# Token-major query/key products in a two-layer hybrid trunk, with the output sums queued behind the low parts

## The chip, the core and the metric

The kernel runs on one core of a Trainium2 chip. A core has a matrix engine (TensorE, PE in the profile, with its weight loads shown apart as PEld), a vector engine (VectorE, DVE), an activation engine (ScalarE, ACT), a general engine (GpSimd, POOL) and a sequencer that here only issues DMAs (SyncE, SP). Each engine takes its instructions in the order of its own queue and waits on semaphores for the others. The metric is the device time of one execution in microseconds; lower is better.

## What is computed

Two layers are applied to x, 512 tokens by 2048 features. Each layer normalises, projects with one wide matrix, runs two groups of heads on the parts of the projection, gates them, maps them back with an output matrix, normalises again and adds to the residual:

```python
h = rmsnorm(x, g_pre)
z = h @ w_in
gq, gk, gv, gg, ga, aq, ak, av, ag = split_columns(z)
log_a = jax.nn.log_sigmoid((ga @ w_alpha + b_alpha)) / GLA_TAU
o_gla = rmsnorm(gla_chunk_causal(gq, gk, gv, log_a)) * jax.nn.silu(gg)
o_att = rmsnorm(chunk_band_attention(aq, ak, av, rel_bias)) * jax.nn.silu(ag)
y = jnp.concatenate([o_gla, o_att], axis=-1) @ w_out
return x + rmsnorm(y, g_post)
```

The attention group has 8 heads of 128 features; a query sees its own 64-token chunk and the eight before it, so with 512 tokens all earlier chunks. The gated linear attention group has 4 heads with 128 key and 256 value features.

## The kernel before

**Operands in two parts.** A float32 operand is split into a rounded high part and the remainder, its low part: ScalarE copies it to the rounded type and VectorE subtracts (`split`). A product is the sum of three matmuls: high by high, high by low, low by high.

**Seven products instead of eight.** The weights come in blocks of 512 columns. A pair of blocks times the tokens is a two by two block product, and `fast_gemm` computes it with seven half-size products named P1 to P7, each over four chunks of 256 rows. The order of the 28 (product, chunk) steps is written out by hand (`PROD`, for the output `PROD_OUT` and `PROD_END`). The operands on the token side are sums of quarters: S1 (for P5), S2 (P6), S3 (P7) and S4 (P3). The operands on the weight side are formed on the way: for P5, P6 and P7 (and P4 of the output) `Job.high` adds or subtracts two weight quarters on VectorE (lines 185 and 187). Then ScalarE makes the high part `wh` (line 191) and VectorE the low part `wl` (line 199). `ahead` loads and prepares three to five steps in advance; `wh` has four buffers, `wl` three and `raw`, into which the weights land, four.

**Products of a layer, in order.** Two gate blocks with a plain product (AG); then by `fast_gemm` AV (values), two query/key pairs (the heads 0 to 3 and 4 to 7), KQ (the linear group's keys and queries), GV, GG, and the output blocks W01 and W23. In layer 0 W23 is a plain product. For a query/key pair (`feature_major=True`) the weights are the stationary operand and 256 tokens the moving one, so the result lies with features on partitions, as the scores want it; for the others 128 tokens are stationary and 512 weight columns moving.

**What fills the gaps.** While products are emitted, a `Pace` steps through a list of generators, `tasks`, at a written rate per step: attention (`attend`), the linear group, transposes of operands, `output_sums`. `until` steps them without a product between when a condition has to hold. A scheduler then sets the order on each engine from a timeline of its own, with the program's order as priority. `tc.issue_after(i)` gives it one more rule: what the block emits on the engine of `i` is queued after `i`, without a semaphore.

**At a query/key product's end** `qk_consume` forms the four results (`combine`, line 338, VectorE, for three; the fourth is read from PSUM as it is) and splits them; both heads of a pair are then handed to `attend`.

**The output product W01.** Its token-side sums are made by `output_sums`: S1 and S2 while GG and the first steps of W01 run, S4 after P5 and P6 have used their first chunks, S3 after their later ones (lines 1136 and 1153 with the splits at lines 105 and 106). `project` (lines 1280 and 1281) takes a finished result's squares on ScalarE and multiplies it by the gain on VectorE.

**The end.** In the last layer the residual of tokens 0 to 255, and of the first half of tile 2 (tokens 256 to 383), is added by a DMA: ScalarE scales the row (line 1305), GpSimd issues an accumulating DMA that adds `x_mid` to it (line 1306), and SyncE stores it (line 1307). The rest is updated by one VectorE instruction with the tokens held in SBUF (line 1311) and stored from SyncE and ScalarE in turn (line 1313).

Of the kernel before, what the change touches and what calls it, by code (L numbers as in the profile page):

```python
# [10 lines left out]
AF = mybir.ActivationFunctionType  # L11
# [22 lines left out]
def hybrid_trunk(  # L34
# [100 lines left out]
    last_cast = [None]  # L135

    class Job:
# [58 lines left out]
        def low(self):  # L196
            self.wl = rtile("wl", dtype=F32R, bufs=3)
            for z in self.parts():
                nc.vector.tensor_tensor(  # L199
                    out=self.wl[:, z, :], in0=self.src[:, z, :], in1=self.wh[:, z, :].bitcast(F32), op=ALU.subtract  # L200
                )
# [114 lines left out]
    def fast_gemm(l, pair, consume, rate=0.0, skip=0, feature_major=False, after=None, end=False, lag=0, ops=A):  # L316
# [38 lines left out]
        def matmuls(job, k, c, ts):  # L355
# [7 lines left out]
            for kk in range(2):  # L363
                if feature_major:
                    for ft in range(4):
                        f = slice(ft * P, (ft + 1) * P)
                        tok = slice(kk * 256, (kk + 1) * 256)
                        dst = out_ps[ft // 2][:, (ft % 2) * 256 : (ft % 2 + 1) * 256]
                        terms = ((job.wh, 0), (job.wh, 1), (job.wl, 0))
                        for m, (lhs, part) in enumerate(terms):  # L370
                            nc.tensor.matmul(  # L371
                                dst, lhs[:, kk, f], a[:, part, tok],
                                start=(fresh and kk == 0 and m == 0 and ft % 2 == 0),
                                stop=(c == 3 and kk == 1 and m == 2), skip_group_check=True,
                            )
                else:
                    for t in ts:
                        tok = slice(kk * 256 + t * P, kk * 256 + (t + 1) * P)
                        terms = ((0, job.wh), (0, job.wl), (1, job.wh))
                        for m, (part, rhs) in enumerate(terms):  # L380
                            nc.tensor.matmul(  # L381
                                out_ps[t], a[:, part, tok], rhs[:, kk, :],
                                start=(fresh and kk == 0 and m == 0),
                                stop=(c == 3 and kk == 1 and m == 2), skip_group_check=True,
                            )
# [302 lines left out]
    def layer(l):  # L688
# [274 lines left out]
        def qk_consume(p):  # L963
            sets = {}

            def f(j, h, b, src, comb):
# [454 lines left out]
```

## Time and profile before

| | us |
|---|---|
| median of three runs | 1648.65 (1648.48 to 1649.47) |
| profiled execution | 1642.34 |
| its span | 1640.5 |
| TensorE busy | 1617.2 |
| VectorE busy | 1253.5 |
| ScalarE busy | 909.7 |
| GpSimd busy | 134.2 |

The span runs from the first to the last instruction of the profiled execution; 1.84 us lie around it. The profiled execution is 6.31 us shorter than the median of the runs. In the trace the stages of a layer stand one after another on TensorE, so that a stretch of time belongs to one product; matmul instructions overlap, and the distance from one start to the next, not the length of one, is what a matmul costs.

### The profile page before, as it was taken

To read this page: it belongs to the slowest core of one execution; us is meant where nothing else is said; L and a number is where in the kernel's file an instruction comes from. 1 tells how busy PE (TensorE), PEld (TensorE's weight loads), DVE (VectorE), ACT (ScalarE), POOL (GpSimd) and SP (SyncE) were. 2 spreads that over 40 slices of the span, in tenths; PEclk is the share of its full clock that TensorE was granted. 3 is DMA by queue.
4 is the path that set the end of the run, shared out by engine and by line. 5 is a ranking of instruction groups with operands and counts; after the bars stand their busy time and mean duration, and the time that the engine had idled before them with its cause. 6 is when DMAs were issued, how large, how long until landed. Compare 5 with 4: busy or idle time off the path is not lost.

```text
span 1640.5 us, 24563 instructions
## 1 busy us (share of the span) xinstructions
PE 1617.2 (99%) x8986; PEld 1383.7 (84%) x8986; DVE 1253.5 (76%) x1635; ACT 909.7 (55%) x1498; POOL 134.2 (8%) x196
## 2 busy tenths in 40 slices
PE   9999999999999999999999999999999999999996
PEld 7888999998888778788888889999988877787885
DVE  5977677687787869985786576776777878699876
ACT  7554445566555456654784444455665545476554
POOL 0120000110100110000132000000000001101002
PEclk9999999999999999999999999999999999999998
DMA  9898685885859667486789486858758596786968
GB/s 345 270 357 293 221 302 199 266 298 173 307 192 339 225 220 267 145 296 214 240 282 394 172 311 218 298 189 273 269 183 291 184 327 235 241 282 246 345 224 269
DMA packets 130760, 426.70 MB, mean 260 GB/s; under 512 B 14084, under 2 KB 26756, under 8 KB 130640
## 3 DMA queue, kind: packets, MB, share of 16 engines
q1 hardware_dynamic: 113760, 366.09, 64.9%
q0 software_dynamic: 16304, 57.96, 9.7%
q8 instruction: 71, 1.16, 0.3%
q10 hardware_dynamic: 576, 1.08, 0.2%
q14 instruction: 49, 0.40, 0.1%
HBM read 371.84 MB, written 53.23 MB: 259 GB/s over the span
## 4 chain that ended last, share of the span: by engine, by line
PE 94%; DMA 2%; DVE 2%; issue 1%; ACT 0%; SPq 0%; DVEq 0%; POOL 0%; ACTq 0%
PE mm L381 47%; PE mm L371 19%; PE mm L302 16%; PE ax L891 2%; PE ax L381 2%; DMA raw<-in_w_dram 1%; PE ax L1072 1%; PE ax L874 1%; PE ax L711 1%; PE ax L1044 1%; DVE wl L199 1%; PE ax L855 1%; PE ax L854 1%; PE ax L853 1%; PE ax L1164 0%
## 5 line engine op out<-in xcount | busy, mean ns | idle before, releaser
L381 PE MATMUL mm<-wh,sa 128*128 128x512 f32 x1472 | 479.2, 396 | 1.2 <-ACT wh L191 1.0
L191 ACT CAST wh<-raw 128x1024 fp32r<-128x1024 f32 (+1 forms) x253 | 265.1, 1052 | 242.6 <-PE mm L381 65.2
L199 DVE TENSOR_TENSOR wl<-raw,wh 128x1024 fp32r<-128x1024 f32 (+1 forms) x253 | 306.5, 1216 | 92.7 <-PE mm L381 38.3
L191 ACT CAST wh<-H 128x1024 fp32r<-128x1024 f32 x240 | 251.4, 1050 | 214.8 <-PE mm L381 90.2
L199 DVE TENSOR_TENSOR wl<-H,wh 128x1024 fp32r<-128x1024 f32 x240 | 292.5, 1221 | 88.1 <-PE mm L381 35.8
L381 PEld LDWEIGHTS mm<-wh,sa 128*128 128x128 f32 x1472 | 277.5, 189 | 68.9 <-issue 7.9
L381 PE MATMUL mm<-wl,sa 128*128 128x512 f32 x736 | 289.6, 394 | 4.7 <-DVE wl L199 4.7
L371 PE MATMUL mm<-sa,wh 128*128 128x256 f32 x1280 | 236.7, 285 | 0.0
L381 PE MATMUL mm<-wh,a 128*128 128x512 f32 x608 | 200.5, 394 | 0.0
L371 PEld LDWEIGHTS mm<-sa,wh 128*128 128x128 f32 x1280 | 199.7, 191 | 0.1
L371 PE MATMUL mm<-sa,wl 128*128 128x256 f32 x640 | 181.2, 283 | 0.0
L381 PEld LDWEIGHTS mm<-wl,sa 128*128 128x128 f32 x736 | 139.1, 189 | 33.7 <-DVE wl L199 6.7
L185 DVE TENSOR_TENSOR H<-H,raw 128x1024 f32<-128x1024 f32 x132 | 160.2, 1219 | 8.1 <-DMA raw<-in_w_dram 7.0
L381 PEld LDWEIGHTS mm<-wh,a 128*128 128x128 f32 x608 | 113.2, 188 | 23.3
L187 DVE TENSOR_TENSOR raw<-H,raw 128x1024 f32<-128x1024 f32 x60 | 73.5, 1224 | 68.8 <-DMA raw<-in_w_dram 68.7
L371 PEld LDWEIGHTS mm<-sa,wl 128*128 128x128 f32 x640 | 122.5, 191 | 0.2
L421 POOL TENSOR_TENSOR sm<-sm,mhalf 128x2 f32<-128x2 f32 (+2 forms) x42 | 57.1, 1360 | 791.8 <-DVE sm L901 453.3
L381 PE MATMUL mm<-wl,a 128*128 128x512 f32 x304 | 119.8, 394 | 0.0
L371 PE MATMUL mm<-a,wh 128*128 128x256 f32 x512 | 95.2, 285 | 0.0
L302 PE MATMUL mm<-wh,a 128*128 128x512 f32 x288 | 91.7, 390 | 0.0
L381 PE MATMUL mm<-wh,g 128*128 128x512 f32 x288 | 90.8, 389 | 0.0
L333 ACT COPY ev<-mm 128x512 f32<-128x512 f32 x96 | 56.0, 583 | 56.3 <-PE mm L381 39.5
(237 smaller groups left out, 2428.5 us busy)
## 6 DMA issues: line engine op xcount, KB each, us to landing
raw<-in_w_dram SPq DMA_DIRECT2D x323, 512.0 KB, 4.8
sa<-S SPq DMA_DIRECT2D x184, 512.0 KB, 4.4
H<-in_w_dram SPq DMA_DIRECT2D x60, 512.0 KB, 4.6
sa<-A SPq DMA_DIRECT2D x48, 512.0 KB, 5.9
S<-g POOLq DMA_DIRECT2D x32, 512.0 KB, 9.0
sa<-oS SPq DMA_DIRECT2D x16, 512.0 KB, 4.5
oa<-g POOLq DMA_DIRECT2D x12, 512.0 KB, 6.6
bias<-in_rel_dram SPq DMA_DIRECT2D x16, 256.0 KB, 4.2
```

The lines of the kernel that those rows point to most:

```text
L185: nc.vector.tensor_tensor(out=h, in0=h, in1=r, op=ALU.add)
L187: nc.vector.tensor_tensor(out=r, in0=h, in1=r, op=ALU.subtract)
L191: last_cast[0] = nc.scalar.copy(self.wh[:, z, :], src[:, z, :]).ins
L199: nc.vector.tensor_tensor(out=self.wl[:, z, :], in0=self.src[:, z, :], in1=self.wh[:, z, :].bitcast(F32), op=ALU.subtract)
L302: nc.tensor.matmul(pss[o], a(part, kk, o) if callable(a) else a[:, part, t], rhs[:, kk, :], start=(i == 0 and kk == 0 and m == 0), stop=(i ...
L333: nc.scalar.copy(e, src[t])
L371: nc.tensor.matmul(dst, lhs[:, kk, f], a[:, part, tok], start=(fresh and kk == 0 and m == 0 and ft % 2 == 0), stop=(c == 3 and kk == 1 and ...
L381: nc.tensor.matmul(out_ps[t], a[:, part, tok], rhs[:, kk, :], start=(fresh and kk == 0 and m == 0), stop=(c == 3 and kk == 1 and m == 2), ...
L421: nc.gpsimd.tensor_tensor(out=out_r, in0=v, in1=mhalf[:, : v.shape[-1]], op=ALU.pow)
L711: nc.tensor.matmul(ps[0:96, half * 256 : (half + 1) * 256], wga[kt // 10][:, kt % 10, :], op[:, i, (kt % 2) * 256 : (kt % 2 + 1) * 256], s ...
L853: nc.tensor.matmul(ps[:, :n], self.qh[:, t], self.kh[:, :n], start=True, stop=False)
L891: nc.tensor.matmul(o, self.pt[i][:, j * P : (j + 1) * P], av[hd // 4, j // 2][:, j % 2, (hd % 4) * P : (hd % 4 + 1) * P], start=(j == 0), ...
```

## The change

- The query/key products lose their own loop: they run like the others, with 128 tokens stationary and 512 weight columns moving. A new task, `turn_qk`, transposes each finished half (eight 128 by 128 transposes into two PSUM tiles) and splits it from PSUM. The fourth result is first copied from PSUM by ScalarE.
- The rates are 2.3 instead of 2.1 in the two query/key products and 2.4 instead of 2.1 in KQ.
- `Job.low` remembers its last instruction in `last_low`. The output sums' VectorE work, and `project` in W01 and most of W23, are queued behind it. S4 waits for later steps (P2 and P5, chunks 2 and 3), S3 also for P3's chunk of its own number.
- In the last layer all of token tile 2 is updated on VectorE. Tokens 0 to 255 keep their accumulating DMA, but each of its four steps is preceded by three empty steps, and the ScalarE scaling is queued behind the last weight cast.

```diff
     def fast_gemm(...)
-                if feature_major:
-                    for ft in range(4):
-                        ...
-                        terms = ((job.wh, 0), (job.wh, 1), (job.wl, 0))
-                        for m, (lhs, part) in enumerate(terms):
-                            nc.tensor.matmul(dst, lhs[:, kk, f], a[:, part, tok], ...)
-                else:
-                    for t in ts: ...
+                for t in ts: ...
     def qk_consume(p):
+            def turn_qk(j, h, z):
+                yield
+                ps = [aux(), aux()]
+                for b in range(2):
+                    for i in range(2):
+                        for t in range(2):
+                            o = i * 256 + t * P
+                            nc.tensor.transpose(
+                                ps[b][:, o : o + P], z[t][:, (2 * b + i) * P : (2 * b + i + 1) * P], ident
+                            )
+                hs = slice(h * 256, (h + 1) * 256)
+                for b in range(2):
+                    hi, lo = sets[j][2 * b][:, :, hs], sets[j][2 * b + 1][:, :, hs]
+                    v = ps[b].rearrange("p (f n) -> p f n", f=2)
+                    if b == 0:
+                        split_scaled(hi, lo, v, -QS)
+                    else:
+                        split(hi, lo, v)
+                if h:
+                    tasks.append(attend(4 * p + 2 * j, sets[j]))
+                yield
...
+                if comb is None:
+                    rows[t] = ev()
+                    nc.scalar.copy(rows[t], src)
                 else:
-                    split(hi, lo, z)
-                if h and b:
-                    tasks.append(attend(4 * p + 2 * j, sets[j]))
+                    rows[t] = comb()
+                if t:
+                    tasks.insert(0, turn_qk(j, h, dict(rows)))
-        fast_gemm(l, PAIRS[1], qk_consume(0), rate=2.1, feature_major=True)
-        fast_gemm(l, PAIRS[2], qk_consume(1), rate=2.1, feature_major=True)
+        fast_gemm(l, PAIRS[1], qk_consume(0), rate=2.3)
+        fast_gemm(l, PAIRS[2], qk_consume(1), rate=2.3)
-        fast_gemm(l, PAIRS[3], kq_consume, rate=2.1)
+        fast_gemm(l, PAIRS[3], kq_consume, rate=2.4)
     def output_sums():
-                with tc.issue_after(last_cast[0]):
+                with tc.issue_after(last_cast[0]), tc.issue_after(last_low[0]):
                     split(op[:, 0, :], op[:, 1, :], src)
-            def sub(dst, a, b):
-                nc.vector.tensor_tensor(out=dst, in0=a, in1=b, op=ALU.subtract)
+            def sub(dst, a, b, op=ALU.subtract):
+                with tc.issue_after(last_low[0]):
+                    nc.vector.tensor_tensor(out=dst, in0=a, in1=b, op=op)
-                    while (("P5", "P6")[i // 2], i % 2 + 2 * (name == "S3")) not in used or (0, OC[i]) not in og:
+                    while (("P2", 2), ("P2", 3), ("P5", 2), ("P5", 3))[i] not in used or name == "S3" and ("P3", i) not in used:
     def finish_token(t, xs):
-                if last and (t < 2 or (t == 2 and i == 0)):
-                    nc.scalar.activation(yt, yt, AF.Copy, scale=r)
+                if last and t < 2:
+                    for _ in range(3):
+                        yield
+                    with tc.issue_after(last_cast[0]):
+                        nc.scalar.activation(yt, yt, AF.Copy, scale=r)
     def out_consume(n):
-                project(o, n + j, comb(t2()), gains[j])
+                with tc.issue_after(last_low[0]) if n == 0 or (j, h) != (0, 1) else nullcontext():
+                    project(o, n + j, comb(t2()), gains[j])
```

45 lines of the change are left out of this document (16 added, 29 removed).

## The prediction

> **What bounds the kernel now.** I read the page's first two parts, then the busy time by stretches cut at the stages' borders, then the chain in order of time, then the timeline where TensorE stops. From the page:
>
> ```profile
> span 1640.5 us, 24563 instructions
> PE 1617.2 (99%) x8986; PEld 1383.7 (84%) x8986; DVE 1253.5 (76%) x1635; ACT 909.7 (55%) x1498; POOL 134.2 (8%) x196
> PEclk9999999999999999999999999999999999999998
> ```
>
> The stretches give length, busy time and instructions of each engine, then the granted TensorE clock and the DMA share. In order: layer 0's AV, its two query/key products, KQ, its W01; layer 1's W01, W23 and what follows its last matmul.
>
> ```profile
> 102.60:178.80 76.20, 76.20 (x338) 63.10 (x337) 56.55 (x51) 34.71 (x37) 1.63 (x3) 1.00 0.83 302
> 178.80:265.40 86.60, 86.60 (x717) 86.30 (x716) 63.26 (x73) 43.07 (x64) 0.00 (x0) 1.00 0.74 252
> 265.40:369.30 103.90, 103.90 (x864) 103.29 (x863) 78.13 (x136) 61.62 (x133) 10.87 (x12) 1.00 0.76 258
> 369.30:467.00 97.70, 97.70 (x503) 82.62 (x502) 71.77 (x105) 60.08 (x115) 7.97 (x7) 1.00 0.69 236
> 648.00:731.50 83.50, 80.66 (x353) 65.33 (x352) 78.42 (x94) 48.73 (x75) 4.84 (x9) 0.98 0.60 205
> 1464.70:1548.70 84.00, 80.78 (x354) 65.55 (x353) 77.84 (x93) 47.83 (x74) 10.13 (x19) 0.98 0.77 276
> 1548.70:1625.00 76.30, 76.30 (x337) 62.86 (x335) 60.36 (x63) 41.19 (x55) 7.89 (x7) 1.00 0.78 251
> 1625.00:1640.50 15.50, 0.00 (x0) 0.00 (x0) 5.81 (x10) 2.29 (x5) 2.40 (x3) 0.65 0.89 289
> ```
>
> TensorE's work is the time: in AV, the query/key products and KQ its busy time is the whole stretch. So there an edit counts by the TensorE time it adds or removes. Two places differ: W01, where TensorE stops, the clock is 0.98, and VectorE is busy 78 of 84 us; and the 15.5 us after the last matmul. The profiled execution (1642.34 us) is the base of the sum; it is 6.31 us below the median, and I carry the difference over to the median unchanged.
>
> **1. The query/key products.** From the chain in order of time, three unbroken runs (start, length, count): a token-major product, a stretch of a feature-major one, a group of transposes.
>
> ```profile
> 102.76 76.16 PE mm L381 x336
> 178.92 65.03 PE mm L371 x542
> 275.38 0.76 PE ax L874 x7
> ```
>
> A 512-wide matmul costs 76.16/336 = 0.2267 us, a 256-wide one 65.03/542 = 0.120, a transpose 0.76/7 = 0.109. A feature-major product has twice the matmuls, 672: 80.6 us against 76.2. Four such products (two in each layer) give back 4 x 4.45 = 17.8. The new turns add 16 x 8 = 128 transposes: 13.9. The third piece is small work put between products. The second query/key stretch has 864 - 672 = 192 such instructions in 103.9 - 80.6 = 23.3 us, 121 ns each; KQ, token-major, has 167 in 97.7 - 76.2 = 21.5, 129 ns each. For the 237 interposed instructions of a layer's two query/key products (45 and 192) and two layers, 8 ns more each is 3.8 at most and nothing at least, since the mixtures differ; I take 1.5. Sum: -17.8 + 13.9 + 1.5 = **-2.4**, ends -3.9 and -0.1.
>
> The Trainium skill, "TensorE: Matmul & The Clock Gate", section "Back-to-back issue gap", gives the isolated spacing at full clock as N/2.4 + 2.5 ns: 216 ns for 512 columns, 109 for 256, 56 for 128. By that, as an estimate, four products save 4 x (73.4 - 72.5) = 3.6 us and the transposes add 7.1, so this part costs 3.5 us and the whole forecast is about 6 us higher. The trace disagrees in the ratio that matters: 0.120 is more than half of 0.2267, and I go by the rows.
>
> What hides the rest of the turns:
>
> ```profile
> L333 ACT COPY ev<-mm 128x512 f32<-128x512 f32 x96 | 56.0, 583 | 56.3 <-PE mm L381 39.5 <-PE mm L371 15.8
> L338 DVE TENSOR_TENSOR ev<-mm,ev 128x512 f32<-128x512 f32 x40 | 27.4, 686 | 7.1 <-PE mm L371 3.7 <-PE mm L381 3.4
> L995 PE MATMUL ax<-cst,ev 128*128 128x128 f32 x32 | 4.5, 272 | 0.0
> ```
>
> The copy of the fourth result is 8 x 0.58 us on ScalarE, which has 40 us free in each of these stretches; the combinations and splits are as many as before. The new wait is TensorE's: a transpose needs the two combinations (0.69 us each), and behind it in the queue stand all products. KQ's query turns (line 995) have the same order of emission and show 0.0 us of idle time ahead of 32 transposes: the scheduler puts other matmuls between. I cost this wait at nothing; without that cover see the first rival. The higher rates give 28 x 0.2 = 5.6 more steps in a product and the turns use 8; KQ has 28 x 0.3 = 8.4 more. They move attention work by a few steps to where TensorE is busy anyway: nothing. Bounds of a shift like that are -0.5 and +1.
>
> **2. W01.** W23 of layer 1 is 336 products and one more in 76.3 us without a stop; W01 has 16 transposes more (1.7), so 84.0 and 83.5 contain 6.0 and 5.5 us of loss. Most of it is one place in each layer, where step 12 (P5, chunk 2) begins (stretches of both layers, then TensorE's and VectorE's timeline in layer 1):
>
> ```profile
> 1498.90:1507.00 8.10, 5.26 (x15) 3.58 (x15) 7.88 (x10) 4.12 (x8) 1.06 (x2) 0.79 0.87 317
> 682.10:690.30 8.20, 5.36 (x18) 3.65 (x17) 8.20 (x11) 4.18 (x8) 0.00 (x0) 0.84 0.48 157
> ...
> 1499.85 0.73 PE L381 MATMUL mm<-wh,sa 128*128 128x512 f32 x2 [0.51 <-ACT wh L191]
> 1502.90 0.50 PE L381 MATMUL mm<-wl,sa 128*128 128x512 f32 x1 [2.33 <-DVE wl L199]
> ...
> 1494.40 0.69 DVE L106 TENSOR_TENSOR g<-g,g 128x512 fp32r<-128x512 f32 x1
> 1495.00 0.69 DVE L106 TENSOR_TENSOR sa<-g,sa 128x512 fp32r<-128x512 f32 x1
> 1495.61 0.69 DVE L1153 TENSOR_TENSOR t<-t,t 128x512 f32<-128x512 f32 x1
> 1496.21 0.69 DVE L1136 TENSOR_TENSOR t<-t,t 128x512 f32<-128x512 f32 x1
> 1496.81 0.69 DVE L106 TENSOR_TENSOR sa<-t,sa 128x512 fp32r<-128x512 f32 x1
> 1497.41 1.22 DVE L185 TENSOR_TENSOR H<-H,raw 128x1024 f32<-128x1024 f32 x1
> 1501.03 0.68 DVE L338 TENSOR_TENSOR t<-ax,ev 128x512 f32<-128x512 f32 x1
> 1501.63 1.22 DVE L199 TENSOR_TENSOR wl<-H,wh 128x1024 fp32r<-128x1024 f32 x1
> ```
>
> Fifteen and eighteen matmuls at 0.2267 us would take 3.4 and 4.1, so 4.7 and 4.1 us are lost: 0.51 + 2.33 of waiting in layer 1, and the rest at a clock of 0.79. VectorE runs five short sums ahead of the addition (line 185) that this step's weights wait for, and a combination ahead of its low part. The edits queue just these behind low parts prepared up to three steps ahead, and S4 starts four steps later, S3 with P3. So this stop should go: -8.8. What is late next is S3: its four sums (two VectorE instructions of 0.69 each) move to steps 16 to 19, each behind a low part that itself waits until its buffer is free, and P3's combinations come on top. Of 5.5 us moved there in each layer I find room for all but about 1 us: between 1507 and 1525 us VectorE works 14.3 of 18.0 (last row below), so 3.7 us are free, and P7 starts four steps after P3, 10.9 us. I take 1.0 of new waiting in each layer: **-6.8**. The ends: -10 if the later small stops go too, and +2 if the moved 5.5 us stay uncovered in both layers (11.0 - 8.8). S4 has six steps (16 us) before P3: hidden. SP's loads wait for low parts and additions to free their buffers, and these come earlier; POOL's stores of the sums come four steps later, ahead of W23, which reads them: hidden.
>
> ```profile
> 1507.00:1525.00 18.00, 18.00 (x81) 14.89 (x80) 14.29 (x15) 12.02 (x16) 2.65 (x5) 1.00 0.74 268
> ```
>
> **3. The end.** Timeline of the last 30 us:
>
> ```profile
> 1611.08 1.16 ACT L1305 ACTIVATE a<-a,sm 128x1024 f32<-128x1024 f32 x1 [2.64 <-POOL sm L421]
> 1617.61 0.85 POOL L1306 DMA_DIRECT2D g<-x_mid  x1
> 1627.18 1.28 DVE L1311 SCALAR_TENSOR_TENSOR g<-g,sm,g 128x1024 f32<-128x1024 f32 x1 [0.17 <-POOL sm L421]
> 1627.82 0.33 SPq L1307 DMA_DIRECT2D out_dram<-g  x1
> 1628.38 1.41 DVE L1311 SCALAR_TENSOR_TENSOR bias<-g,sm,bias 128x512 f32<-128x512 f32 x2
> 1628.70 0.88 POOL L1306 DMA_DIRECT2D g<-x_mid  x1 [1.04 <-ACT g L1305]
> 1629.70 1.41 DVE L1311 SCALAR_TENSOR_TENSOR sg<-g,sm,sg 128x512 f32<-128x512 f32 x2
> 1636.66 0.33 SPq L1307 DMA_DIRECT2D out_dram<-g  x1
> ```
>
> The last event is tile 2's first half: an accumulating DMA from 1628.70, stored from 1636.66, landed at 1640.5. On VectorE it costs one more 1.28 us ahead of the four short updates: the last of those ends at 1631.11 + 1.2 = 1632.3, and with the 3.84 us that the last store took the span ends at 1636.2, 4.3 earlier. Against that, the four earlier accumulations start later. Twelve empty steps, three to a product step of 12 x 0.2267 = 2.72 us, put the fourth scaling up to 10.9 us later in the program; but the first one ran only at 1611.08, when GpSimd's root was there, so most of that delay is already in the old times, and I take 2.5 us of it as real. The fourth accumulation was issued at 1617.61 and its store at 1627.82; 2.5 us later that store lands at 1630.3 + 3.84 = 1634.2, before the new end, but the DMA share is already 0.89 and the stores share it. I take **-3.0**, ends -4.3 and 0. Queued behind the ScalarE scaling is what ends the last projections (their squares): at 1.14 to 1.16 us a scaling they are hidden as long as the fourth one runs before the last matmul.
>
> **Sum.** -2.4 - 6.8 - 3.0 = -12.2: 1630.1 for the profiled execution, 1636.4 for the median.
>
> **The rivals.**
> *TensorE waits at the turns (slower).* If transposes are queued close behind their product, each of 16 turns waits for two combinations and a low part ahead of them: up to 1.37 + 1.22 = 2.6 us. It decides from 12.2/16 = 0.76 us a turn; at 1.5 us, 24 us, the time is 1660. For: turns are inserted at the head of the task list, and they take two of four small PSUM tiles. Against: line 995's row. Chance 0.14.
> *The stop in W01 moves.* S3 behind the low parts stops P7 as P5 stopped before: -2.4 + 0 - 3 gives 1643.3. For: VectorE's 78 of 84 us. Against: its free 3.7 us. Chance 0.20.
> *Nothing to be measured*: the turns eat part 1, the stop moves, and the end is held by the later accumulations: about 1648. Chance 0.04.
> *The clock falls at the transposes.* At the stop above the clock fell, and 4.7 - 2.84 = 1.9 us of layer 1's loss came from it; 16 turns at that price are 30 us, so 1666. Against: the second query/key stretch, full of interposed transposes, has a clock of 1.00. Chance 0.02. The Trainium skill, "TensorE: Matmul & The Clock Gate", section "Part 4: PE-mode transpose", says that transposes do not count as activity for the clock, which is what this rival needs; the trace shows no sign of it.
>
> **How the numbers follow.** The forecast has the remaining 0.60. The measurement can tell about 0.2%, 3.3 us: faster is below 1645.3. Forecast and moved stop lie there but for a few in a hundred each: faster 0.74; same 0.10; slower 0.16, the waits, the clock and a part of the moved stop with the worse end of part 2. The ends of the parts add up to -18.7 and +2.9, so 1630 to 1651.6; of that and the rivals I leave out what lies above 1650, most of the first rival among it: 1630 to 1650. By itself the likeliest case spans 1631 to 1641.
>
> **What would show it.** Right: query/key stretches of 82 to 86 and 99 to 104 us with clock 1.00; no idle time before the turns; W01 near 79 to 81 us and no wait for `wl` at P5; the last store issued near 1632 and a tail of 11 to 13 us. Wrong: TensorE idle released by VectorE's combinations in the turns; a wait of P7 on S3 or on a low part at steps 20 to 24; stores of tokens 0 to 255 as the last event.

## The result

The changed kernel takes 1649.47 us (median of 12 runs, 1646.31 to 1655.08); the kernel before, run beside it on the same chips, 1647.42 (1644.08 to 1649.79). The ratio is 1.0017, with a 95% interval of 1.0005 to 1.003: slightly slower, where 12 us less was forecast. Its profiled execution took 1647.76 us and is the one read here. It is 5.4 us longer than that of before, but the medians differ by 2.05 only: the profiled execution of before was 5.1 us below its median and this one 1.7, so the two traces show a larger loss than the runs do. From its page:

```profile
span 1646.0 us, 22105 instructions
PE 1617.0 (98%) x7770; PEld 1323.9 (80%) x7770; DVE 1257.3 (76%) x1636; ACT 915.3 (56%) x1505; POOL 127.0 (8%) x195
PEclk9999999999999999999999999999999999999998
```

TensorE has 1216 instructions fewer and is as busy as before, but the busy time overlaps itself, so the stretches tell more. Cut at the same stage borders: layer 0's AV, its two query/key products, KQ, GV and W01, then layer 1's W01, W23 and what follows the last matmul.

```profile
102.30:179.20 76.90, 76.47 (x338) 62.92 (x337) 58.65 (x54) 36.34 (x40) 2.17 (x4) 1.00 0.87 315
179.20:263.00 83.80, 83.80 (x394) 69.78 (x393) 62.57 (x71) 41.27 (x57) 0.00 (x0) 1.00 0.77 264
263.00:366.70 103.70, 103.69 (x554) 87.96 (x554) 78.64 (x137) 62.48 (x132) 8.71 (x12) 1.00 0.72 241
366.70:465.70 99.00, 98.33 (x505) 83.15 (x504) 72.45 (x101) 62.02 (x117) 4.36 (x6) 1.00 0.74 250
465.70:557.80 92.10, 91.01 (x441) 71.71 (x441) 71.99 (x97) 47.94 (x78) 8.31 (x8) 1.00 0.69 248
650.50:733.50 83.00, 80.64 (x354) 65.49 (x353) 77.92 (x93) 48.12 (x74) 4.64 (x9) 0.98 0.59 202
1469.40:1553.60 84.20, 79.83 (x354) 63.93 (x352) 76.21 (x92) 47.55 (x74) 10.21 (x19) 1.00 0.72 259
1553.60:1630.90 77.30, 77.09 (x337) 62.73 (x336) 61.95 (x64) 41.85 (x56) 9.38 (x7) 1.00 0.79 258
1630.90:1646.00 15.10, 0.02 (x1) 0.00 (x0) 7.03 (x11) 1.17 (x4) 1.55 (x2) 0.67 0.88 297
```

GV, which the prediction did not look at, was this before (same view):

```profile
467.00:555.30 88.30, 88.30 (x421) 69.33 (x420) 71.30 (x91) 45.34 (x69) 5.17 (x7) 1.00 0.73 261
```

The reader sees three things. The query/key products end about where they were forecast (83.8 and 103.7 us), but GV has grown by 3.8 us and 20 TensorE instructions. From the first query/key product to the end of GV layer 0 takes 2.1 us more than before, layer 1 1.8 us. W01 is where it was. The tail is 0.4 us shorter instead of 3 or more. The rest of the 5.4 us lies in layer 1's W23 (+1.0) and in stretches whose code did not change: AV has 0.7 us more here, and over the executions of this study its length wanders between 76.2 and 78.0 us. Layer 1's W23 wanders too (76.3 before, 78.4 in e1, with the old code there), and so does W01 where its code is unchanged (82.9 to 84.2 us in layer 0, 83.6 to 84.7 in layer 1, over before, e1, e3, e4, e5 and e12). A difference of 1 us in one of these stages, in one trace, shows nothing by itself. All ratios below are against the kernel before, run beside each kernel.

### The profile page after: what moved, and what is told of

Same layout as the page of the kernel before. It is cut to its first block, busy times and chain, and to the rows that moved or that the text cites. A ratio compares the mean times of both kernels' runs of the same rounds, so it can differ in the third digit from the quotient of the medians.

```text
span 1646.0 us, 22105 instructions
## 1 busy us (share of the span) xinstructions
PE 1617.0 (98%) x7770; PEld 1323.9 (80%) x7770; DVE 1257.3 (76%) x1636; ACT 915.3 (56%) x1505; POOL 127.0 (8%) x195
## 4 chain that ended last, share of the span: by engine, by line
PE 87%; DMA 5%; DVE 4%; issue 1%; ACT 1%; POOL 0%; SPq 0%; DVEq 0%; ACTq 0%; POOLq 0%
PE mm L368 60%; PE mm L302 16%; DMA raw<-in_w_dram 4%; PE ax L878 2%; DVE wl L199 2%; PE ax L368 2%; PE ax L1079 1%; PE ax L698 1%; PE ax L1051 1%; PE ax L960 1%; DMA sa<-S 1%; PE ax L861 1%; PE ax L842 1%; PE ax L841 1%; PE ax L840 1%
## 5 line engine op out<-in xcount | busy, mean ns | idle before, releaser
L368 PE MATMUL mm<-wh,sa 128*128 128x512 f32 x2112 | 682.9, 395 | 6.9 <-DVE sa L106 4.6
L368 PEld LDWEIGHTS mm<-wh,sa 128*128 128x128 f32 x2112 | 394.2, 188 | 99.8 <-issue 7.7
L368 PE MATMUL mm<-wl,sa 128*128 128x512 f32 x1056 | 414.1, 393 | 1.3 <-DVE wl L199 1.3
L199 DVE TENSOR_TENSOR wl<-raw,wh 128x1024 fp32r<-128x1024 f32 (+1 forms) x253 | 305.7, 1214 | 76.4 <-PE mm L368 39.7
L368 PE MATMUL mm<-wh,a 128*128 128x512 f32 x864 | 283.7, 395 | 0.0
L368 PEld LDWEIGHTS mm<-wl,sa 128*128 128x128 f32 x1056 | 198.8, 188 | 41.6 <-DVE wl L199 2.2
L185 DVE TENSOR_TENSOR H<-H,raw 128x1024 f32<-128x1024 f32 x132 | 160.6, 1220 | 15.0 <-DMA raw<-in_w_dram 13.3
L368 PE MATMUL mm<-wl,a 128*128 128x512 f32 x432 | 170.6, 395 | 0.0
L368 PEld LDWEIGHTS mm<-wl,a 128*128 128x128 f32 x432 | 81.2, 188 | 16.6
L302 PE MATMUL mm<-wh,a 128*128 128x512 f32 x288 | 91.7, 390 | 0.0
L368 PE MATMUL mm<-wh,g 128*128 128x512 f32 x288 | 90.8, 390 | 0.0
L302 PE MATMUL mm<-wh,g 128*128 128x512 f32 x240 | 81.8, 391 | 0.0
L204 DVE TENSOR_TENSOR H<-H,raw 128x1024 f32<-128x1024 f32 x48 | 58.6, 1221 | 22.7 <-DMA raw<-in_w_dram 22.5
L302 PE MATMUL mm<-wh,sa 128*128 128x512 f32 x224 | 72.9, 391 | 0.8 <-ACT wh L191 0.8
L368 PEld LDWEIGHTS mm<-wh,g 128*128 128x128 f32 x288 | 53.9, 188 | 11.5 <-ACT wh L191 0.4
```

The source lines that it names most:

```text
L185: nc.vector.tensor_tensor(out=h, in0=h, in1=r, op=ALU.add)
L199: last_low[0] = nc.vector.tensor_tensor(out=self.wl[:, z, :], in0=self.src[:, z, :], in1=self.wh[:, z, :].bitcast(F32), op=ALU.subtract).ins
L204: nc.vector.tensor_tensor(out=h, in0=h, in1=self.src, op=ALU.add)
L302: nc.tensor.matmul(pss[o], a(part, kk, o) if callable(a) else a[:, part, t], rhs[:, kk, :], start=(i == 0 and kk == 0 and m == 0), stop=(i ...
L368: nc.tensor.matmul(out_ps[t], a[:, part, tok], rhs[:, kk, :], start=(fresh and kk == 0 and m == 0), stop=(c == 3 and kk == 1 and m == 2), ...
```

## Experiments on the query/key products

**The three pieces of part 1 without the rest** (e1) is the kernel before with the first half of the change's diff: the loop removed, `turn_qk` and its copy, the new rates.

```diff
     def qk_consume(p):
+            def turn_qk(j, h, z):
+                ...
+                if t:
+                    tasks.insert(0, turn_qk(j, h, dict(rows)))
-        fast_gemm(l, PAIRS[1], qk_consume(0), rate=2.1, feature_major=True)
+        fast_gemm(l, PAIRS[1], qk_consume(0), rate=2.3)
...
```

> The kernel before with the token-major query/key products, their turns and the new rates alone. Theory A (the loss lies here: attention falls behind and its rest runs in GV with TensorE waiting for it): from the last KQ product's end on nothing changes, the two query/key stretches become about 3 us shorter in each layer together, KQ 1 us and GV 3 to 4 us longer, and the time is 3 to 5 us above before. Rival B (this part alone gains its 2.4 us as forecast, and the loss comes from its meeting with the other parts): 1 to 3 us below before, GV no more than 1 us longer.

Measured: 1650.19 us, ratio 1.0018 (1.0008 to 1.0029), +3.0 us. Part 1 alone makes a loss as large as the whole change's, and GV grows just as in the changed kernel: 92.0 us in layer 0, again with 441 TensorE instructions.

**Products without turns** (e5): the products become token-major, but the results go on through the old `qk_consume`.

```diff
-        fast_gemm(l, PAIRS[1], qk_consume(0), rate=2.1, feature_major=True)
+        fast_gemm(l, PAIRS[1], qk_consume(0), rate=2.3)
-        fast_gemm(l, PAIRS[2], qk_consume(1), rate=2.1, feature_major=True)
+        fast_gemm(l, PAIRS[2], qk_consume(1), rate=2.3)
-        fast_gemm(l, PAIRS[3], kq_consume, rate=2.1)
+        fast_gemm(l, PAIRS[3], kq_consume, rate=2.4)
```

> Token-major query/key products with the new rates, but without the turns: the finished 512-column results are split and handed to the scores as they lie, untransposed (left out: 128 transposes and 8 copies; the scores then multiply the wrong elements, in the same number and shape). Theory A (the products give what was counted, and the turns cost more than eight transposes): 13 to 17 us below before, and the kernel with turns alone (the first run) 17 to 21 us above this one, 1.1 to 1.3 us for each of 16 turns where 0.87 was counted. Rival B (the products give less, because small work between 512-wide matmuls is dearer than between 256-wide ones): 6 to 10 us below before, and a turn costs 0.7 to 0.9 us.

Measured: 1628.95 us, ratio 0.9895 (0.9879 to 0.991): -17.3 us, of 17.8 counted, with an interval of -14.8 to -19.9. The saving of the products is real. (From the first query/key product to the end of GV, both layers together, the two traces differ by 14.8 us; that of before lies well below its median.) Layer 0's two query/key products, KQ and GV in e5:

```profile
178.50:261.70 83.20, 82.79 (x383) 68.74 (x382) 63.54 (x74) 42.82 (x62) 0.00 (x0) 1.00 0.76 263
261.70:360.60 98.90, 98.90 (x515) 84.13 (x514) 76.34 (x134) 60.99 (x129) 9.61 (x12) 1.00 0.78 263
360.60:461.20 100.60, 100.60 (x528) 85.51 (x527) 75.52 (x113) 63.08 (x124) 6.39 (x7) 1.00 0.70 238
461.20:546.70 85.50, 84.94 (x406) 67.68 (x405) 70.22 (x86) 44.77 (x66) 6.09 (x7) 1.00 0.76 267
```

The turns therefore cost 0.9895 against 1.0018, 20.2 us (18.4 when these four stages of both layers are added up in the profiled executions of e1 and e5): 1.26 us for each of 16, where the prediction had 13.9 + 1.5 = 15.4, or 0.96. Layer 0's GV is 6.5 us longer (92.0 against 85.5), since with the turns in, attention reaches into GV with 35 TensorE instructions more. Much of that is moved work and not loss: KQ is 2.4 us shorter in e1 (98.2 against 100.6).

**Each turn twice** (e12) asks what the transposes themselves cost, by repeating each one in e1's kernel.

```diff
-                            nc.tensor.transpose(
-                                ps[b][:, o : o + P], z[t][:, (2 * b + i) * P : (2 * b + i + 1) * P], ident
-                            )
+                            for _ in range(2):
+                                nc.tensor.transpose(
+                                    ps[b][:, o : o + P], z[t][:, (2 * b + i) * P : (2 * b + i + 1) * P], ident
+                                )
```

> The first run (token-major query/key products, nothing else) with every transpose of a turn issued twice, 128 more. Theory A (a transpose costs its 0.109 us, and the rest of a turn's price is waiting and switching): 13 to 15 us above the first run. Rival B (a transpose in this place costs the whole price found, 20.2 us for 128): 18 to 22 us above it.

Measured: 1661.02 us, ratio 1.0092 (1.0079 to 1.0105), 12.2 us above e1: 0.095 us for each of the 128. The counted 0.109 was a fair price: e12 also lost the two waits in GV that are shown next, 2.2 us in e1, so that its transposes may cost 14.4 us, 0.113 each. So of the turns' 20.2 us some 12 to 14 are the transposes, and 6 to 8 are something else. The groups of the changed kernel say that it is not a wait at the turns (line 960 is `turn_qk`'s transpose, line 878 a transpose of `attend`, and the idle time just before is the column behind the second bar):

```profile
L960 PE MATMUL ax<-cst,ev 128*128 128x128 f32 x128 | 19.4, 273 | 0.7 <-DVE ev L338 0.7
L878 PE MATMUL ax<-g,t 128*128 128x128 f32 x320 | 46.3, 275 | 2.2 <-ACT t L884 2.2
```

In 128 transposes TensorE stood idle for 0.7 us in all on the combinations (line 338). The 2.2 us are one place in each layer, in GV, where the last head of attention has nothing between its own steps (TensorE's timeline, layer 0):

```profile
480.29 0.83 PE L878 MATMUL ax<-g,t 128*128 128x128 f32 x6
480.96 0.60 PE L903 MATMUL ax<-cst,sg 128*128 128x128 f32 x4
482.65 0.71 PE L878 MATMUL ax<-g,t 128*128 128x128 f32 x4 [1.09 <-ACT t L884]
```

Before, layer 0's GV had no idle time at all (88.30 us busy of 88.30). Attention does start later: its first transpose at line 878 (line 891 before) comes 82.0 us after layer 0's first query/key product begins, where it was 75.3 before. The waits come to 2.9 us of the 6 to 8, and that is the most they can explain: e5, without turns, has one of 1.28 us inside attention as well (in layer 1's second query/key product). What the rest is, dearer interposed work or short waits below the view's grain, stays open.

**More steps** (e8) is e1 with the rates 2.8, 2.8 and 2.6, so that attention does not run late into GV.

```diff
-        fast_gemm(l, PAIRS[1], qk_consume(0), rate=2.3)
+        fast_gemm(l, PAIRS[1], qk_consume(0), rate=2.8)
-        fast_gemm(l, PAIRS[2], qk_consume(1), rate=2.3)
+        fast_gemm(l, PAIRS[2], qk_consume(1), rate=2.8)
-        fast_gemm(l, PAIRS[3], kq_consume, rate=2.4)
+        fast_gemm(l, PAIRS[3], kq_consume, rate=2.6)
```

> The kernel of the first run (token-major query/key products with turns) with more steps: rate 2.8 in the query/key products and 2.6 in KQ. Theory A (part of the loss is attention left over for GV, where it runs with nothing between): GV back to 88 us, no 1.1 us wait for the squares there, 2 to 4 us below the first run, so near before. Rival B (the small work costs the same wherever it stands): within 1 us of the first run.

Measured: 1648.64 us, ratio 1.0015 (1.0006 to 1.0025). Layer 0's second query/key product became 6 us shorter than in e1 (97.6), KQ 4 us longer (101.8), GV stayed (92.6, with 459 TensorE instructions), and W01 took 87.6. Theory A's sign, GV back at 88, did not come: attention was not moved out of GV, so this run does not test what its place there costs. The four stages are 3.3 us shorter together in layer 0 and W01 is 4.3 longer; why W01 grows was not looked into. In all, another pace moves the work from one product to the next and wins nothing that these intervals can tell from e1.

## Experiments on W01

**Part 2 alone** (e2): `last_low`, the output sums and `project` queued behind it, and the new conditions of S4 and S3.

```diff
-            def sub(dst, a, b):
-                nc.vector.tensor_tensor(out=dst, in0=a, in1=b, op=ALU.subtract)
+            def sub(dst, a, b, op=ALU.subtract):
+                with tc.issue_after(last_low[0]):
+                    nc.vector.tensor_tensor(out=dst, in0=a, in1=b, op=op)
...
-                    while (("P5", "P6")[i // 2], i % 2 + 2 * (name == "S3")) not in used or (0, OC[i]) not in og:
+                    while (("P2", 2), ("P2", 3), ("P5", 2), ("P5", 3))[i] not in used or name == "S3" and ("P3", i) not in used:
...
-                project(o, n + j, comb(t2()), gains[j])
+                with tc.issue_after(last_low[0]) if n == 0 or (j, h) != (0, 1) else nullcontext():
+                    project(o, n + j, comb(t2()), gains[j])
```

> The kernel before with the output sums and the projections queued behind the low parts, and with the new conditions for S4 and S3, alone. Theory A (the stop only moves from P5 to P7): W01 within 1 us of 83.5 and 84.0 in the two layers, no wait for a low part at step 12, waits for S3's split (line 106 into an sa tile) at steps 20 to 23, time within 1.5 us of before. Rival B (the forecast held for this part, and W01 of the changed kernel was spoilt by other parts): W01 near 80.5, time 5 to 7 us below before.

Measured: 1646.08 us, ratio 1.0000 (0.9986 to 1.0014). W01 takes 83.2 and 84.8 us. The largest of TensorE's waits in layer 1's W01 in e2, and then all over 0.3 us in the same stage of the changed kernel:

```profile
1535.81 0.97 PE L381 MATMUL mm<-wh,sa 128*128 128x512 f32 x3 [1.77 <-DVE sa L106]
```

```profile
1507.95 0.74 PE L368 MATMUL mm<-wh,sa 128*128 128x512 f32 x2 [0.78 <-ACT wh L191]
1514.94 0.50 PE L368 MATMUL mm<-wl,sa 128*128 128x512 f32 x1 [0.62 <-DVE wl L199]
1529.45 0.97 PE L368 MATMUL mm<-wh,sa 128*128 128x512 f32 x3 [0.61 <-DVE sa L106]
1536.99 0.98 PE L368 MATMUL mm<-wh,sa 128*128 128x512 f32 x3 [1.79 <-DVE sa L106]
1541.07 0.98 PE L368 MATMUL mm<-wh,sa 128*128 128x512 f32 x3 [0.56 <-DVE sa L106]
```

The 2.33 us on a low part at step 12 is gone in both. In its place stand three waits on the splits of S3 (line 106), 2.96 us in the changed kernel (1.09, 1.77 and 0.60 in e2), and two smaller ones on weights, 1.40. Layer 0 of the changed kernel has one wait of 1.61 us on a split of S3 and one of 0.69 on a low part. VectorE's timeline ahead of the largest shows why:

```profile
1533.92 0.68 DVE L338 TENSOR_TENSOR t<-mm,ev 128x512 f32<-128x512 f32 x1
1534.53 0.68 DVE L1144 TENSOR_TENSOR t<-t,t 128x512 f32<-128x512 f32 x1
1535.12 1.22 DVE L185 TENSOR_TENSOR H<-H,raw 128x1024 f32<-128x1024 f32 x1
1536.26 0.68 DVE L106 TENSOR_TENSOR sa<-g,sa 128x512 fp32r<-128x512 f32 x1
```

VectorE works without a gap (it is busy for 18.00 of 18 us from 1519 to 1537), and the split that P7 needs stands behind a combination, a subtraction and an addition for later weights.

**Which piece of part 2 does it?** e7 queues only the sums behind the low parts and keeps the old conditions; e6 queues `project` too, in W01 and W23.

```diff
 # e7 and e6: last_low, the splits and sub() of output_sums as in the change, the old `while`
 # e6 besides:
-                project(o, n + j, comb(t2()), gains[j])
+                with tc.issue_after(last_low[0]) if n == 0 or (j, h) != (0, 1) else nullcontext():
+                    project(o, n + j, comb(t2()), gains[j])
```

> As the run before, but the projections stay unqueued: only the sums are behind the low parts. Theory A: within 1.5 us of the run before, since the five sums ahead of the addition at step 12 are what counted. Rival B (the combination ahead of the low part counted as well): 2 us or more slower than the run before, with a wait for a low part at step 12 left.

> The kernel before with the output sums and the projections queued behind the low parts, but with the old conditions for S4 and S3. Theory A (the queueing removes the stop at step 12, the late S3 makes the new ones): no waits for an S3 split at steps 20 to 23, W01 79 to 81.5 us in both layers, 5 to 9 us below before in all. Rival B (VectorE is full, so any order stops TensorE somewhere): W01 within 1 us of 83.5 and 84.0.

Measured: e7 1648.42 us, ratio 1.0015 (1.0003 to 1.0026); e6 1645.63 us, ratio 0.9991 (0.9982 to 1.0000). With the sums alone the stop stays (2.19 and 2.57 us on a low part), and W01 takes 83.5 and 86.6 us. With the projections queued as well it takes 81.5 and 83.4:

```profile
651.60:733.10 81.50, 79.93 (x353) 64.08 (x352) 78.24 (x93) 49.52 (x75) 4.31 (x8) 1.00 0.59 208
1469.80:1553.20 83.40, 79.85 (x354) 64.08 (x353) 76.81 (x92) 47.93 (x74) 10.16 (x19) 1.00 0.76 279
```

In layer 0 the wait is down to 0.60 us; in layer 1 one of 1.95 remains. So the order of the projections mattered and that of the sums by itself did not. In size e6 falls between its theories: 81.5 us is the upper end of A, 83.4 belongs to B, and the whole gained 1.5 us where A had 5 to 9. The intervals do not tell e6 with the old conditions (0.9991) from e2 with the new ones (1.0000).

**Order or load?** e13 takes the multiplications of `project` in W01 off VectorE, eight instructions in each layer, and keeps the old order; e14 is e13 with e6's edit.

```diff
-            nc.vector.tensor_tensor(
-                out=ys[o, n // 2][:, (n % 2) * W : (n % 2 + 1) * W], in0=src, in1=gp, op=ALU.mult
-            )
+            dst = ys[o, n // 2][:, (n % 2) * W : (n % 2 + 1) * W]
+            if n > 1:
+                nc.vector.tensor_tensor(out=dst, in0=src, in1=gp, op=ALU.mult)
+            else:
+                nc.scalar.copy(dst, src)
```

> The kernel before, with the eight multiplications by the gain in W01 left out: ScalarE copies the projected rows instead (the gain of the first 1024 output features is left out of the result). 5.5 us less on VectorE in each layer, nothing on GpSimd. Theory A (W01 is bound by the load of VectorE): W01 80 to 81.5 us in both layers, 4 to 7 us below before. Rival B (it is the order at step 12): W01 within 1 us of 83.5 and 84.0, the wait for a low part at step 12 unchanged at 2.3 us.

> The same leaving out, with the sums and projections queued behind the low parts under the old conditions for S4 and S3 (the sixth run's edit). Theory A (load): like the run before or 1 us better. Rival B (order, with the load deciding what is late next): 2 to 4 us better than the sixth run and clearly better than the run before, W01 79 to 80.5 us.

Measured: e13 1644.5 us, ratio 0.9989 (0.9975 to 1.0002); e14 1639.7 us, ratio 0.9957 (0.9944 to 0.9971). W01 of e13 in layer 0, then of e14 in both layers:

```profile
647.70:731.50 83.80, 80.43 (x353) 65.61 (x352) 75.39 (x88) 51.48 (x81) 5.39 (x10) 0.98 0.62 209
```

```profile
649.80:729.60 79.80, 78.99 (x354) 64.41 (x353) 74.97 (x87) 52.13 (x81) 5.37 (x10) 1.00 0.62 224
1463.50:1546.40 82.90, 79.36 (x353) 64.31 (x353) 73.79 (x86) 51.46 (x81) 10.69 (x20) 1.00 0.79 285
```

Less load in the old order leaves W01 as long as it was, with a wait of 1.7 us where there were 2.33. The same load in the new order brings layer 0 to 79.8 us, where the forecast had it; the order opens the stop there, and the load decides how much comes back later. In layer 1 a wait of 1.92 us on a low part stays in e14, as in e6. VectorE's timeline ahead of it, in e14, shows that it is not VectorE's load:

```profile
1498.14 1.23 DVE L185 TENSOR_TENSOR H<-H,raw 128x1024 f32<-128x1024 f32 x1 [2.05 <-DMA raw<-in_w_dram]
1499.29 1.22 DVE L199 TENSOR_TENSOR wl<-H,wh 128x1024 fp32r<-128x1024 f32 x1
```

VectorE itself stands idle for 2.05 us until the weights of the next step's addition have landed, and the low part that TensorE waits for is queued behind this addition. e6 (2.08 us) and e7 (2.10) have the same idle time in layer 1 ahead of the same step; layer 0 of e6 has none there. Why these weights land late in layer 1 was not looked into. Of the 0.0034 between e6 and e14, 5.6 us, W01 gives 2.2; layer 1's W23 shows 1.9 more (76.4 against 78.3), which is within what that stage wanders by itself.

**The same load on GpSimd** (e9): the subtractions and additions of the output sums and W01's multiplications run on `nc.gpsimd` instead of `nc.vector`, nothing else.

```diff
             def sub(dst, a, b):
-                nc.vector.tensor_tensor(out=dst, in0=a, in1=b, op=ALU.subtract)
+                nc.gpsimd.tensor_tensor(out=dst, in0=a, in1=b, op=ALU.subtract)
...
-            nc.vector.tensor_tensor(
+            (nc.vector if n > 1 else nc.gpsimd).tensor_tensor(
```

> The kernel before, with 16 sums of the output product and the 8 multiplications by the gain in W01 moved in each layer from VectorE to GpSimd (24 x 0.69 = 16.5 us off VectorE, of which some 13 in W01); no other edit. Theory A (W01 is bound by a full VectorE, and queueing alone cannot help): W01 79 to 81 us in both layers, the waits for low parts there mostly gone, 4 to 9 us below before. Rival B (it is the order alone, not the load): W01 within 1 us of 83.5 and 84.0, or the same stop with GpSimd as its releaser.

Measured: 1672.95 us, ratio 1.0166 (1.0153 to 1.0179). W01 takes 95.6 and 98.1 us, and VectorE is busy longer in it than before (87.69 us with 77 instructions in layer 0, against 78.42 with 94). It could not answer the question on load, for a reason told at the end.

## Experiments on the end

**Part 3 alone** (e3) is the change's edit of `finish_token`, with three empty steps and the queueing behind the last cast. **Without that delay** (e4) it is this:

```diff
-                if last and (t < 2 or (t == 2 and i == 0)):
+                if last and t < 2:
                     nc.scalar.activation(yt, yt, AF.Copy, scale=r)
```

> The kernel before with the changed end alone. Theory A (the DMA engines are full from the first accumulation on, so the end is set by when that starts and by the bytes): 2.6 us fewer of accumulation, the first one starting 1 to 2 us later against the last matmul, net 0.5 to 1.5 us shorter from last matmul to end. Rival B (VectorE's chain sets the end, as forecast): 3 to 4 us shorter.

> As the run before, but without the empty steps and without queueing the scaling behind the last cast, so that the accumulations start when they did before. Theory A: the full 2.6 us of the accumulation that is gone, a tail of 12.5 to 13.2 us, 1 to 2 us better than with the delay. Rival B: the same as with the delay, since VectorE's chain ends both.

Measured: e3 1644.05 us, ratio 0.9987 (0.9974 to 1.0001); e4 1641.77 us, ratio 0.9974 (0.9961 to 0.9987). The stretch after the last matmul, in e3 and in e4:

```profile
1627.90:1640.80 12.90, 0.05 (x1) 0.00 (x0) 7.05 (x11) 1.20 (x4) 1.55 (x2) 0.65 0.85 307
```

```profile
1626.70:1638.93 12.23, 0.00 (x0) 0.00 (x0) 7.00 (x11) 1.14 (x4) 1.52 (x2) 0.71 0.85 317
```

Against 15.5 before, the edit alone gives 2.6 us and without the delay 3.3; in the changed kernel it gave 0.4. The 2.6 lies between what the two theories of e3 had, and the delay cost 0.7 us where theory A of e4 had 1 to 2. The end of the changed kernel, from GpSimd's accumulations (line 1317) over SyncE's stores of them (line 1318) to the last stores of the updated rows (line 1324):

```profile
1620.18 0.97 POOL L1317 DMA_DIRECT2D a<-x_mid  x1 [1.49 <-ACT a L1316]
...
1626.13 0.85 POOL L1317 DMA_DIRECT2D g<-x_mid  x1
...
1635.95 0.33 SPq L1318 DMA_DIRECT2D out_dram<-g  x1
1636.37 0.42 SPq L1324 DMA_DIRECT2D out_dram<-g  x1
1636.83 1.41 DVE L1322 SCALAR_TENSOR_TENSOR sg<-g,sm,sg 128x512 f32<-128x512 f32 x2
...
1638.17 1.10 SPq L1324 DMA_DIRECT2D out_dram<-sg  x1
```

And the same end in e3:

```profile
1615.59 0.97 POOL L1309 DMA_DIRECT2D a<-x_mid  x1 [1.49 <-ACT a L1308]
...
1631.10 0.33 SPq L1310 DMA_DIRECT2D out_dram<-g  x1
...
1633.86 1.41 DVE L1314 SCALAR_TENSOR_TENSOR sg<-g,sm,sg 128x512 f32<-128x512 f32 x2
1634.63 0.33 SPq L1316 DMA_DIRECT2D out_dram<-sg  x1
```

VectorE's last update ends at 1638.24 in the changed kernel and at 1635.27 in e3, 7.3 and 7.4 us after the last matmul: no difference. The accumulations start 10.7 us before the last matmul in the changed kernel, 12.3 in e3. Each takes its time on DMA engines that are busy to 0.88 and 0.85 of the stretch, so the store of the last one is issued 5.05 and 3.2 us after the last matmul, and the final stores, which share the engines with it, land 7.8 and 5.5 us after VectorE's end. Length times rate gives, as an estimate, what is moved after the last matmul: 15.1 us at 297 GB/s, 4.5 MB, in the changed kernel, 15.5 at 289, also 4.5, before, 4.0 in e3 (12.9 at 307) and 3.9 in e4 (12.23 at 317). At rates so near each other the length of these ends goes by the bytes that are left when TensorE stops. That has a limit: e15, below, has 3.1 MB left (12.13 us at 255) and an end as long as e4's.

**Why do they start later?** e11 is the changed kernel with the projections queued in W01 only; e15 is the changed kernel with the scaling neither delayed nor queued behind the cast.

```diff
 # e11
-                with tc.issue_after(last_low[0]) if n == 0 or (j, h) != (0, 1) else nullcontext():
+                with tc.issue_after(last_low[0]) if n == 0 else nullcontext():
 # e15
-                    for _ in range(3):
-                        yield
-                    with tc.issue_after(last_cast[0]):
-                        nc.scalar.activation(yt, yt, AF.Copy, scale=r)
+                    nc.scalar.activation(yt, yt, AF.Copy, scale=r)
```

> The changed kernel, with the projections queued behind the low parts in W01 only and no longer in W23. Theory A (that queueing makes tokens 0 to 255 ready 1.7 us later and so eats the gain of the end): from last matmul to end 12.7 to 13.5 us where the changed kernel has 15.1, 2 to 3 us below the changed kernel. Rival B (the end is longer for another reason): 14.5 to 15.5 us, no difference.

> The changed kernel without the empty steps and without queueing the scaling behind the last cast. Theory A (the end is set by when the accumulations start, since the DMA engines are full from there): from last matmul to end 13 to 14 us where the changed kernel has 15.1, 1 to 2.5 us below the changed kernel. Rival B: 14.6 to 15.5 us, no difference.

Measured: e11 1650.0 us, ratio 1.0029 (1.0017 to 1.0041), with a tail of 15.26: the projections of W23 are not the cause. e15 1648.86 us, ratio 1.0012 (1.0001 to 1.0023). Its W23 and its tail, and the largest wait in that W23:

```profile
1555.50:1636.40 80.90, 79.12 (x337) 63.73 (x336) 62.12 (x64) 42.08 (x56) 8.47 (x7) 0.98 0.82 262
1636.40:1648.53 12.13, 0.00 (x0) 0.00 (x0) 6.98 (x11) 1.12 (x4) 1.52 (x2) 0.66 0.70 255
```

```profile
1628.22 0.73 PE L368 MATMUL mm<-wh,g 128*128 128x512 f32 x2 [1.03 <-ACT wh L191]
```

The tail is short again, but W23 loses 3.6 us, because scalings now stand ahead of the last weight casts on ScalarE. In this kernel the delay protects the casts and costs the end nearly as much. In the changed kernel and in e3 the first scaling waits 2.64 us for GpSimd's root, not for a cast, and the root for the sum of the row on VectorE, which runs 15.7 us before the last matmul in the changed kernel (1615.24) and 17.3 in e3: the 1.6 us are there already. What is left as a cause is the weights: VectorE waits for the last blocks to land (line 187) in every version, but in the changed kernel the last two of these waits, 1.77 and 0.45 us, end 24.8 and 20.9 us before the last matmul, in e3 28.5 and 26.0. That the row's sum is late because of them is argued only, and why these weights land later stays open.

**Part 2 at its best with part 3** (e10): e6's order with the projections queued in W01 only, and e4's end; the query/key products and the conditions of S4 and S3 stay as before.

```diff
 # last_low, the splits and sub() of output_sums as in the change, finish_token as in e4, and
-                project(o, n + j, comb(t2()), gains[j])
+                with tc.issue_after(last_low[0]) if n == 0 else nullcontext():
+                    project(o, n + j, comb(t2()), gains[j])
```

> The kernel before with two of the edits: sums queued behind the low parts with the old conditions and W01's projections queued too (those of W23 not), and the undelayed end. Theory A (parts add up): 1.5 us from W01 and 4 us from the end, 1640 to 1642 where before is 1646. Rival B (the queueing of W23's projections gave part of the gain of the sixth run): 2 to 3 us below before.

Measured: 1641.41 us, ratio 0.9975 (0.9964 to 0.9986), W01 81.2 and 83.7 us, tail 12.75. It beats both kernels, and so does e4 with an edit of one line and the same time within the intervals.

## Why the prediction was wrong, step by step

**Part 1: -2.4 forecast, +3.0 measured.** The four products' 17.8 us held (17.3 in e5). By the rule in the Trainium skill, "TensorE: Matmul & The Clock Gate", section "Back-to-back issue gap", the same four products would, as an estimate, have saved 3.6 us; e5 decides for the trace's rows. The estimate for the part by that rule, +3.5, lies near the measured +3.0 by luck, from two terms that are each far off. The transposes' 13.9 held too (12.2 in e12). "I cost this wait at nothing" nearly held: the wait at the turns is 0.7 us, the precedent of line 995 was right, and the rival that put the loss there is wrong as to the place. The step that failed is the shift of attention, "to where TensorE is busy anyway: nothing", bounded by +1: the turns cost 4.8 us more than 13.9 + 1.5. Of that, 2.2 us are shown as waits at the far end, in GV, where attention, which starts later with its operands turned first, runs out of products to hide behind. Where the rest is lost stays open. The signs that the prediction named for this part (83.8 and 103.7 us, a clock of 1.00, hardly any idle time before the turns) came true all the same; none of them looked at GV.

**Part 2: -6.8 forecast, 0.0 measured in e2.** The stop at step 12 went, as said. The mis-sized term is the 1.0 us of new waiting in each layer: in the changed kernel it is 2.30 us in layer 0 and 4.36 in layer 1, 1.61 and 2.96 of it on the splits of S3, and W01 as a whole came out as long as with the stop. The free 3.7 us of VectorE was an average over a stretch of 18 us in the old order; the queue ahead of one split is what counts, and there it had no gap. This is the second rival, the moved stop, to which I gave 0.20.

**Part 3: -3.0 forecast, -0.4 in the changed kernel, -2.6 by itself.** VectorE's chain ended 7.3 us after the last matmul, as forecast (1632.3 - 1625.0). The store of the last accumulated rows was issued 5.05 us after the last matmul, near the forecast's 5.3 (1630.3 - 1625.0). The term that failed is the 3.84 us for the last store: it took 7.8, because the store of the accumulated rows, which was thought to land before, was issued only 2.3 us ahead of VectorE's end and shared the DMA engines with the last stores. In e3, where it was issued 3.2 us after the last matmul, the term was 5.5.

**The rest.** The clock stayed at 1.00 in the stretches full of transposes; that rival fell, and with it, here, the use of the Trainium skill's sentence on transposes (same page, "Part 4: PE-mode transpose"). What came true as a whole is the rival with a chance of 0.04, "Nothing to be measured", in all of its three parts and nearly in its time: 1648 against 1649.47. Measured alone, the parts give +3.0, 0.0 and -2.1 us, +0.9 in all; the whole gave +2.8, and the difference is no larger than the intervals.

## What to carry to other kernels

An edit that puts a new step ahead of a long chain costs its instructions, which can be counted, and the lateness of that chain where it ends, which is read several stages on: look there for what still hides it. In a stage where an engine works without a gap, a new order of its queue can open one stop and make the next, and behind a stop that is gone the next limit may be another (here the weights' landing); cut the load as well, or look at the queue in front of each wait instead of the free time of a stretch. At the end of this kernel the last stores shared the DMA engines with what was left of earlier transfers, so the start of the earlier transfers counts as much as the last instruction.

## What the runs showed of the hardware

GpSimd is no free place for VectorE's work. The low parts of layer 1's W01 before and in e9, then a group of GpSimd's subtractions in e9 (one of that shape took VectorE 0.69 us):

```profile
L199 DVE TENSOR_TENSOR wl<-H,wh 128x1024 fp32r<-128x1024 f32 x16 | 19.5, 1221 | 1.9 <-ACT wh L191 1.8
```

```profile
L199 DVE TENSOR_TENSOR wl<-H,wh 128x1024 fp32r<-128x1024 f32 x16 | 27.2, 1709 | 2.7 <-ACT wh L191 2.7
...
L1136 POOL TENSOR_TENSOR g<-g,g 128x512 f32<-128x512 f32 x5 | 7.7, 1538 | 0.0
```

GpSimd takes 1.5 us for what VectorE does in 0.69, and VectorE's own subtractions grow by 40% (1709 against 1221 ns) in a stage in which GpSimd is busy for 44.5 of 98.1 us. The Trainium skill, "SBUF — State Buffer", section "Who interferes with whom", says that a VectorE instruction with two SBUF inputs contends with a GpSimd instruction that reads SBUF; the rows agree.

An accumulating transfer took longer than the stores beside it: in the changed kernel the last one was issued at 1626.13 and could be stored only at 1635.95, 9.8 us for 512 KB. Medians from issue to landing in the last 28 us, for two accumulations and three stores of the same size:

```profile
g<-x_mid POOLq DMA_DIRECT2D x2, 512.0 KB, 7.6
...
out_dram<-g SPq DMA_DIRECT2D x3, 512.0 KB, 4.3
```

The other two accumulations (into `a`) have a median of 6.5, the stores of their rows 5.2. That the adding itself is what takes longer is not shown: two plain loads of `x_mid` into `g`, issued by GpSimd in layer 1's W01, have a median of 9.1.
